# Sixteen experts on one core: fixed program order for experts 0 to 14, overflow branch in front of the first

## The chip, the core and the metric

The kernel runs on one core of a Trainium2 chip. The metric is device time in us for one launch, both layers. An engine is named as the profile names it: PE is TensorE (PEld its weight loads), ACT ScalarE, DVE VectorE, POOL GpSimd, SP SyncE, which here only issues transfers; a q behind a name is that engine's sequencer.

## What is computed

The reference is a trunk of two layers over 512 positions of width 1024, in float32. Each layer has a mixer (projections, attention to 256 memory tokens, an output projection, a norm) and then a mixture of 16 experts, of which each position uses two, and a second norm:

```
for i in range(DEPTH):
    ...
    x = layer_norm(ALPHA * x + o, ln1_g[i], ln1_b[i])
    f = grouped_moe(x, router_w, router_b, w_gate[i], w_up[i], w_down[i])
    x = layer_norm(ALPHA * x + f, ln2_g[i], ln2_b[i])

def grouped_moe(...):
    ...                       # top-2 of 16 experts per position, weights in combine
    for e in range(N_EXPERTS):
        h = jax.nn.silu(xt @ w_gate[e]) * (xt @ w_up[e])      # 1024 -> 512
        out = out + combine[:, e:e + 1] * (h @ w_down[e])     # 512 -> 1024
```

## The kernel before

**Mixer and routing.** Each layer first does its mixer and the routing. Routing leaves on chip, per expert, the rows that it takes (`idxs`, L633), their weights (`gates`, L634), and a count of experts with more than 128 rows (`overflow`, L598: `cnt` on TensorE, then four small operations on VectorE up to `nover`, L609).

**One expert** (`experts`, from L649). GpSimd gathers up to 128 rows of x from HBM (L667, two buffers `xg`). TensorE transposes them (`xtrans`, eight blocks, L676), ScalarE and VectorE split the result into a high and a low part (`split_to`, L207 and L208: `xgt`). `gate_up` makes ga and ua: 48 matmuls in the order ga, ua, ga, ua, twelve each. A product of float32 is three matmuls (`mm3`, L202 to L204): high by high, low weights by high x, high weights by low x. Then silu on ScalarE (L692) and the product with ua on VectorE (L693) give h. `htrans` transposes h (`htr`, L699), splits it (`ht`), and `down` makes 24 matmuls into ya in two halves; each half is scaled by the gate on ScalarE (`evict`, L714) into y, which GpSimd adds to the result in HBM (L663).

In the loop over e, expert e's gate and up stand first, then the transposes of e+1, then the down of e-1, then htr of e. Expert 0 has no down behind its gate and up.

**Weights** (`Stream`). Six loads of 1 MB per expert (gate, up, gate, up and two of down) come through SyncE (L147) into a ring of raw pages, at most four in flight. ScalarE copies a raw page to `high` (L168) and VectorE subtracts (`low`, L169), into a ring of eight split pages, ten from expert 5 on, when the raw pages fall from 11 to 9 in layer 0 and from 13 to 11 in layer 1. A load into a raw page is issued once VectorE's `low` has read what was in it; a split is made once TensorE has used up the pages it goes into.

**What sets the order.** A scheduler puts the instructions of each engine into a sequence, by its own model of their times. An engine works its sequence off in order, so an instruction that waits holds up all that stand behind it on that engine.

**The branch** (`more`, L886 on). An expert with more than 128 rows gets the rest of them in a loop under `tc.If(n > 0)`; n is `nover`. All five engines load the number (L889) and compare it (L890); those that skip the body catch up on its semaphores. In the executions shown here the body was not run. Before, the call stands in the loop behind gate and up of expert 0, the transposes of expert 1 and the gather of expert 3; it has a page `rest` of its own.

The functions that the diff touches:

## Time and profile before

| what | value |
|---|---|
| median of 3 runs | 1063.36 us (1061.95 to 1065.77) |
| the profiled execution | 1063.26 us, span 1061.6 us |
| mean granted TensorE clock | 0.970 |
| first ga of the experts in layer 0, in layer 1 | 219.41 us, 733.36 us |

The span runs from the first to the last instruction on the chip; the execution's own time is 1.7 us longer. All times of the rows below are counted from the span's start. Matmuls are pipelined: how far apart two of them start says what one costs, and a matmul's own duration is longer.

### The profile page before, as it was taken

What the parts mean: (1) busy time and instruction counts of PE and PEld (TensorE: products, weight loads), DVE (VectorE), ACT (ScalarE), POOL (GpSimd) and SP (SyncE); (2) the same over time, 40 slices, a digit from 0 to 9 for tenths busy, and PEclk for the clock granted to TensorE, in tenths of its full rate; (3) what the DMA queues carried; (4) which work ended last, traced back from release to release, by engine and by line L of the source; (5) the groups of instructions that cost most, each with busy time, mean ns of one, the idle gap of its engine ahead of it and who ended that gap; (6) DMA issues with size and microseconds to landing.
All of it is one profiled execution on the core that took longest, in us unless ns stands there. A gap on an engine that the chain in (4) does not pass through costs nothing. (4 is left out here: it accounts for less than half of the span.)

```text
span 1061.6 us, 12769 instructions
## 1 busy us (share of the span) xinstructions
PE 991.3 (93%) x4815; PEld 812.6 (77%) x4816; DVE 780.7 (74%) x880; ACT 628.6 (59%) x682; POOL 170.8 (16%) x115
## 2 busy tenths in 40 slices
PE   8999999769999999899899999986699999998995
PEld 6788889658888887678679887875588888886873
DVE  4638667866889976788794656475789999777885
ACT  4526533446788865767653514232688888767762
POOL 0000004311222212101101000212022222221123
PEclk9999999979999999999999999986899999999998
DMA  9713358568999999999690414492499999999934
GB/s 323 274 41 119 120 198 296 181 224 287 361 371 307 396 350 330 319 319 338 175 390 26 159 51 159 148 390 74 172 362 349 371 341 376 354 356 335 333 67 157
DMA packets 102220, 273.31 MB, mean 257 GB/s; under 512 B 10442, under 2 KB 10966, under 8 KB 102152
## 3 DMA queue, kind: packets, MB, share of 16 engines
q1 hardware_dynamic: 89480, 242.84, 62.8%
q0 software_dynamic: 11808, 26.97, 9.1%
q10 hardware_dynamic: 864, 2.62, 0.7%
q8 instruction: 39, 0.64, 0.2%
q14 instruction: 29, 0.24, 0.1%
HBM read 262.22 MB, written 26.21 MB: 272 GB/s over the span
## 5 line engine op out<-in xcount | busy, mean ns | idle before, releaser
L169 DVE TENSOR_TENSOR low<-raw,high 128x2048 fp32r<-128x2048 f32 x189 | 429.8, 2290 | 90.6 <-ACT high L168 87.2
L168 ACT ACTIVATE high<-raw 128x2048 fp32r<-128x2048 f32 x189 | 358.2, 1913 | 44.8 <-PE ga L204 33.4
L168 ACT ACTIVATE split<-raw 128x1024 fp32r<-128x1024 f32 x66 | 68.5, 1058 | 76.5 <-PE za L204 26.0
L203 PE MATMUL ua<-low,xgt 128*128 128x512 f32 x248 | 97.8, 394 | 9.0 <-DVE low L169 9.0
L202 PE MATMUL ya<-high,ht 128*128 128x512 f32 x256 | 103.5, 406 | 1.3 <-ACT high L168 1.3
L203 PE MATMUL ya<-low,ht 128*128 128x512 f32 x256 | 102.3, 400 | 2.1 <-DVE low L169 2.1
L204 PE MATMUL ya<-high,ht 128*128 128x512 f32 x256 | 101.8, 398 | 0.8 <-DVE ht L208 0.7
L203 PE MATMUL ga<-low,xgt 128*128 128x512 f32 x248 | 99.9, 403 | 2.1 <-DVE low L169 1.9
L202 PE MATMUL ga<-high,xgt 128*128 128x512 f32 x248 | 100.4, 405 | 0.0
L204 PE MATMUL ga<-high,xgt 128*128 128x512 f32 x248 | 98.1, 396 | 0.0
L169 DVE TENSOR_TENSOR split<-raw,split 128x1024 fp32r<-128x1024 f32 x57 | 68.7, 1221 | 39.7 <-ACT split L168 38.9
L202 PE MATMUL ua<-high,xgt 128*128 128x512 f32 x248 | 97.4, 393 | 0.1
L204 PE MATMUL ua<-high,xgt 128*128 128x512 f32 x248 | 96.9, 391 | 0.0
L667 POOL DMA_INDIRECT xg<-x1d,idxs x32 | 49.8, 1556 | 267.6 <-PE xt L676 238.3
L169 POOL TENSOR_TENSOR split<-raw,split 128x1024 fp32r<-128x1024 f32 x9 | 21.7, 2406 | 284.8 <-DVE sto L474 148.9
L207 ACT ACTIVATE xgt<-xt 128x512 fp32r<-128x512 f32 x64 | 36.4, 592 | 50.3 <-PE ua L203 26.0
L202 PE MATMUL za<-xh,split 128*128 128x512 f32 x160 | 61.9, 393 | 2.0 <-ACT xh L207 2.0
L203 PEld LDWEIGHTS ua<-low,xgt 128*128 128x128 f32 x248 | 46.6, 188 | 21.0 <-DVE low L169 11.7
L203 PE MATMUL za<-xl,split 128*128 128x512 f32 x160 | 62.5, 391 | 0.0
L204 PE MATMUL za<-xh,split 128*128 128x512 f32 x160 | 61.5, 390 | 0.0
L203 PEld LDWEIGHTS ya<-low,ht 128*128 128x128 f32 x256 | 48.6, 190 | 13.7 <-DVE low L169 3.1
L202 PEld LDWEIGHTS ya<-high,ht 128*128 128x128 f32 x256 | 48.6, 190 | 12.9 <-ACT high L168 1.8
(250 smaller groups left out, 1899.1 us busy)
## 6 DMA issues: line engine op xcount, KB each, us to landing
raw<-in_w_gate_dram SPq DMA_DIRECT2D x64, 1024.0 KB, 8.8
raw<-in_w_up_dram SPq DMA_DIRECT2D x64, 1024.0 KB, 8.3
raw<-in_w_down_dram SPq DMA_DIRECT2D x64, 1024.0 KB, 9.5
raw<-in_w_kv_dram SPq DMA_DIRECT2D x8, 1024.0 KB, 7.0
raw<-in_w_out_dram SPq DMA_DIRECT2D x8, 1024.0 KB, 6.1
raw<-in_w_in_b_dram SPq DMA_DIRECT2D x8, 1024.0 KB, 10.2
raw<-in_w_in_a_dram SPq DMA_DIRECT2D x6, 1024.0 KB, 5.5
x1d<-x POOLq DMA_DIRECT2D x8, 512.0 KB, 5.8
```

What stands on the lines that cost most here:

```text
L168: act.activation(high, src, AF.Copy)
L169: (pool_e if self.on_pool(self.count) else vec).tensor_tensor(low, src, high, op=OP.subtract)
L202: pe.matmul(o, a[0], b[0], start=start, stop=False)
L203: pe.matmul(o, a[0], b[1], start=False, stop=False)
L204: return pe.matmul(o, a[1], b[0], start=False, stop=stop)
L207: r = act.activation(hi, src, AF.Copy)
L667: pool_e.indirect_dma_start(out=xg[:, e % 2], out_offset=None, in_=x1d[i], in_offset=bass.IndirectOffsetOnAxis(ap=tabs[e][0], axis=0), bou ...
```

## The change

The call of `more` moves to a place ahead of the rings, the first transposes and the loop; instead of the page `rest` it uses the page `hy`, which the experts write later. In the loop, TensorE, ScalarE and VectorE work experts 0 to 14 in the order in which the program is written (`tc.manual_schedule`); before the last expert's gate and up the scheduler takes over again. So that the written order is usable, three pieces change place in the program: silu stands behind the last release of ga's pages, the product ahead of the last release of ua's (a release is what emits the next split), and the eviction of a half of down ahead of the release of its last page.

```diff
--- before.py
+++ after.py
@@ -688,9 +688,11 @@
                             k = 4 * half + 2 * j + kk
                             m = mm3(a[u], (xt[:, 0, k, :], xt[:, 1, k, :]), (g[:, 0, kk, :], g[:, 1, kk, :]),
                                     k == 0, k == KB - 1)
+                        if half and u and j:
+                            vec.tensor_tensor(hp[:, 1, :], hp[:, 0, :], a[1], op=OP.mult)
                         W.done(g)
-            act.activation(hp[:, 0, :], a[0], AF.Silu)
-            vec.tensor_tensor(hp[:, 1, :], hp[:, 0, :], a[1], op=OP.mult)
+                    if half and not u:
+                        act.activation(hp[:, 0, :], a[0], AF.Silu)
             return m
 
         def htrans(e):
@@ -707,8 +709,9 @@
                     for kk in range(2):
                         k = 2 * j + kk
                         mm3(o, (ht[:, 0, k, :], ht[:, 1, k, :]), (g[:, 0, kk, :], g[:, 1, kk, :]), k == 0, k == 3)
+                    if j:
+                        evict(n, o)
                     W.done(g)
-                evict(n, o)
 
         def scaled(e):
             return lambda n, o: act.activation(ys[e % 2][:, n * 512:(n + 1) * 512], o, AF.Copy, scale=tabs[e][1])
@@ -719,23 +722,23 @@
             with tc.issue_after(last_entry[-1]):
                 keep_warm(8)
         fill()
-        rest = page("more", [P, 4, FE])
+        more(i, hy)
         W.keep, W.flight = 0, 4
         W.ahead, W.whole, W.on_pool = 6, True, lambda n: False
         W.rings(8)
         W.pump()
         xtrans(0)
         gather(2)
+        order = ExitStack()
+        order.enter_context(tc.manual_schedule(engines={ET.PE, ET.Activation, ET.DVE}))
         for e in range(E):
+            if e == last:
+                order.close()
             up = gate_up(e, (lambda: (down(last - 1, scaled(last - 1)), scatter(last - 1))) if e == last else None)
             if e + 1 < E:
                 xtrans(e + 1)
             if e + 3 < E:
                 gather(e + 3)
-            if e == 0:
-                more(i, rest)
-                drop(rest)
-                W.pump()
             if e == 5:
                 W.parts += 2
             if 0 < e < last:
```

**VectorE in layer 0, ahead of the first expert** (`split` is a half page of the mixer's last weights, `low` the low part of an expert's weights, `vt` a part of attention's values). Before:

```order
L169 TENSOR_TENSOR split_1868<-raw_1225,split_1868 128x1024
L208 TENSOR_TENSOR vt_1701<-va,vt_1701 128x512
L633 TENSOR_SCALAR idxs<-tab 128x16
L634 TENSOR_REDUCE gates<-tab 128x16
L604 TENSOR_TENSOR ovf<-cnt,thr 1x48
L607 TENSOR_REDUCE ovn<-ovf 1x1
L608 CAST flags<-ovf 1x48
L609 CAST nover<-ovn 1x1
L169 TENSOR_TENSOR low_1931<-raw_1310,high_1930 128x2048
L208 TENSOR_TENSOR vt_1701<-va,vt_1701 128x512
L169 TENSOR_TENSOR low_1894<-raw_1254,high_1893 128x2048
L208 TENSOR_TENSOR xgt_1693<-xt,xgt_1693 128x512 x2
```

and now:

```order
L169 TENSOR_TENSOR split_1868<-raw_1225,split_1868 128x1024
L169 TENSOR_TENSOR low_2040<-raw_1254,high_2039 128x2048
L633 TENSOR_SCALAR idxs<-tab 128x16
L634 TENSOR_REDUCE gates<-tab 128x16
L208 TENSOR_TENSOR vt_1701<-va,vt_1701 128x512 x2
L169 TENSOR_TENSOR low_2081<-raw_1310,high_2080 128x2048
L604 TENSOR_TENSOR ovf<-cnt,thr 1x48
L607 TENSOR_REDUCE ovn<-ovf 1x1
L608 CAST flags<-ovf 1x48
L609 CAST nover<-ovn 1x1
L892 TENSOR_LOAD nover
```

The two splits of expert weights stood behind `nover`; one of them now stands ahead of `idxs`, the other ahead of the count.

**TensorE in layer 0 where the branch was, behind expert 0's gate and up.** Before, the first and the last rows of the branch:

```order
L204 MATMUL ua<-high_1930,xgt_1693 128x512
L676 MATMUL xt<-ident,xg_1690 128x128 x4
L889 TENSOR_LOAD nover
L890 COMPARE_AND_BRANCH
...
L890 UNCONDITIONAL_BRANCH
L699 MATMUL htr<-ident,h_1692 128x128 x4
L202 MATMUL ga<-high_1948,xgt_1693 128x512
```

and now:

```order
L204 MATMUL ua<-high_2080,xgt_1693 128x512
L676 MATMUL xt<-ident,xg_1690 128x128 x8
L701 MATMUL htr<-ident,h_1692 128x128 x4
L202 MATMUL ga<-high_2098,xgt_1693 128x512
L203 MATMUL ga<-low_2099,xgt_1693 128x512
```

The load of `nover` and the branch left this place (they stand ahead of expert 0's eight transposes now), and all eight transposes of expert 1 stand here, where four of them stood earlier.

**ScalarE in layer 0 at experts 10 and 11** (the rows of before are those at 441 to 462 us). Before:

```order
L714 ACTIVATE h_1692<-ya,gates 128x512
L168 ACTIVATE high_3659<-raw_3466 128x2048
L207 ACTIVATE ht<-htr 128x512
L714 ACTIVATE h_1692<-ya,gates 128x512
L168 ACTIVATE high_3697<-raw_3484 128x2048
L168 ACTIVATE high_3717<-raw_3502 128x2048
L168 ACTIVATE high_3748<-raw_3520 128x2048
L207 ACTIVATE xgt_1693<-xt 128x512
L168 ACTIVATE high_3766<-raw_3558 128x2048
L692 ACTIVATE h_1692<-ga 128x512
L207 ACTIVATE xgt_1693<-xt 128x512
L168 ACTIVATE high_3784<-raw_3578 128x2048
```

and now, for one expert:

```order
L717 ACTIVATE h_1692<-ya,gates 128x512
L168 ACTIVATE high_3699<-raw_3485 128x2048
L717 ACTIVATE h_1692<-ya,gates 128x512
L168 ACTIVATE high_3719<-raw_3503 128x2048
L207 ACTIVATE ht<-htr 128x512
L168 ACTIVATE high_3749<-raw_3523 128x2048
L168 ACTIVATE high_3767<-raw_3560 128x2048
L168 ACTIVATE high_3785<-raw_3580 128x2048
L695 ACTIVATE h_1692<-ga 128x512
L168 ACTIVATE high_3805<-raw_3610 128x2048
L207 ACTIVATE xgt_1693<-xt 128x512 x2
```

Between two evictions stands one split, and `ht` comes behind both; the order is the same for each expert. VectorE's order follows it: six splits, the product and `ht` between one expert's `xgt` and the next's.

## Rows read from the trace of the kernel before

**Rows 1.** The page's table of engines: busy us, share of the span, instructions.

```profile
PE 991.3 (93%) x4815; PEld 812.6 (77%) x4816; DVE 780.7 (74%) x880; ACT 628.6 (59%) x682; POOL 170.8 (16%) x115
```

**Rows 2.** Busy time by stage in layer 0's expert loop (from:to in us, length; then busy us and instructions of TensorE, its weight loads, VectorE, ScalarE and GpSimd, the granted clock, the DMA engines' busy share, GB/s).

```profile
340.00:400.00 60.00, 60.00 (x284) 49.70 (x283) 50.73 (x34) 45.47 (x40) 13.93 (x7) 1.00 1.01 369
420.00:480.00 60.00, 53.97 (x244) 42.46 (x244) 44.80 (x27) 43.00 (x36) 6.82 (x5) 1.00 0.95 320
```

**Rows 3.** TensorE in layer 0 around its first expert, in order of time (start, duration, both us; in brackets the idle time before it and what ended it; a matmul's duration reaches into the next one's).

```profile
214.19 1.95 PE L676 MATMUL xt<-ident,xg 128*128 128x128 f32 x8 [3.87 <-DMA xg<-x1d,idxs]
...
219.41 0.77 PE L202 MATMUL ga<-split,xgt 128*128 128x512 f32 x1
...
231.74 0.63 PE L676 MATMUL xt<-ident,xg 128*128 128x128 f32 x4
237.97 1.09 PE L699 MATMUL htr<-ident,h 128*128 128x128 f32 x4 [5.59 <-DVEq L890]
238.71 0.78 PE L202 MATMUL ga<-high,xgt 128*128 128x512 f32 x1
```

**Rows 4.** The same in layer 1.

```profile
730.90 2.81 PE L676 MATMUL xt<-ident,xg 128*128 128x128 f32 x12 [1.96 <-DMA xg<-x1d,idxs]
733.36 0.78 PE L202 MATMUL ga<-split,xgt 128*128 128x512 f32 x1
...
754.41 1.09 PE L699 MATMUL htr<-ident,h 128*128 128x128 f32 x4 [7.14 <-DVEq L890]
```

**Rows 5.** The chain that ended last, behind the branch of layer 1 (start, us, what; here a matmul's time is the distance to the next).

```profile
755.50 0.43 PE ga L202
...
758.84 0.23 PE ga L202
```

**Rows 6.** What TensorE waited for in 240 to 512 (the first two rows) and in 755 to 1010 (the last two): us in total, times, longest.

```profile
PE ua L203 <- DVE low L169: 5.1, 3, 1.8
...
PE ya L202 <- ACT high L168: 1.3, 1, 1.3
...
PE ua L203 <- DVE low L169: 2.7, 2, 1.7
PE ga L203 <- DVE low L169: 1.0, 2, 0.5
```

**Rows 7.** VectorE and GpSimd ahead of layer 0's first expert: the table of rows, the count of overflows, the first gather.

```profile
209.75 0.16 DVE L633 TENSOR_SCALAR idxs<-tab 128x16 int32<-128x16 f32 x1
...
210.81 0.14 DVE L609 CAST nover<-ovn 1x1 int32<-1x1 f32 x1
...
210.20 1.09 POOL L667 DMA_INDIRECT xg<-x1d,idxs  x1 [1.15 <-DVE gates L634]
```

**Rows 8.** The branch's own instructions in both layers, on TensorE and SyncE (durations in ns: least, median, most; start of the first and of the last), and SyncE's next weight load behind it in layer 0.

```profile
L889 PEldq TENSOR_LOAD <-nover x2: 315/403/491, 228.6 to 744.5; - x2
...
L889 SPq TENSOR_LOAD <-nover x2: 283/372/462, 237.6 to 729.7; - x2
...
L890 PEldq COMPARE_BRANCH  x2: 318/336/353, 229.2 to 745.0; - x2
...
243.18 0.38 SPq L147 DMA_DIRECT2D raw<-in_w_up_dram  x1
```

**Rows 9.** ScalarE in layer 1 during the first expert: the second split, and the table load ahead of silu.

```profile
740.19 1.92 ACT L168 ACTIVATE high<-raw 128x2048 fp32r<-128x2048 f32 x1 [0.33 <-DVE low L169]
...
744.74 1.28 ACT L692 ACT_TABLE_LOAD   x1
```

**Rows 10.** Groups of ScalarE and VectorE in 240 to 510 (count; busy us, mean ns; idle time before them and what ended it).

```profile
L168 ACT ACTIVATE high<-raw 128x2048 fp32r<-128x2048 f32 x84 | 159.0, 1913 | 18.2 <-PE ga L204 13.3 <-PE ua L204 4.9
...
L714 ACT ACTIVATE h<-ya,gates 128x512 f32<-128x512 f32 x14 | 9.6, 689 | 7.6 <-PE ya L204 7.6
...
L169 DVE TENSOR_TENSOR low<-raw,high 128x2048 fp32r<-128x2048 f32 x83 | 188.6, 2290 | 40.6 <-ACT high L168 39.0 <-DMA raw<-in_w_gate_dram 0.8 <-DMA raw<-in_w_down_dram 0.5
L208 DVE TENSOR_TENSOR xgt<-xt,xgt 128x512 fp32r<-128x512 f32 x28 | 18.6, 684 | 0.7 <-ACT xgt L207 0.7
```

**Rows 11.** Transfers: in 340 to 400 the queue of the weight loads (packets, MB, share of 16 engines) and one kind of load (count, KB each, median us to landing), in 430 to 480 another kind, in 850 to 950 all packets and the queue of the weight loads.

```profile
q1 hardware_dynamic: 6702, 19.93, 87.9%
...
raw<-in_w_up_dram SPq DMA_DIRECT2D x6, 1024.0 KB, 11.5
...
raw<-in_w_down_dram SPq DMA_DIRECT2D x6, 1024.0 KB, 7.1
...
DMA packets 12601, 35.79 MB, mean 358 GB/s; under 512 B 1318, under 2 KB 1318, under 8 KB 12595
...
q1 hardware_dynamic: 10867, 32.04, 86.1%
```

**Rows 12.** ScalarE in layer 0 around 446, in order of time.

```profile
445.62 0.60 ACT L207 ACTIVATE ht<-htr 128x512 fp32r<-128x512 f32 x1 [1.90 <-PE ya L203]
...
446.69 5.51 ACT L168 ACTIVATE high<-raw 128x2048 fp32r<-128x2048 f32 x3
```

**Rows 13.** TensorE's htr of three experts of layer 0, six experts apart.

```profile
276.08 0.60 PE L699 MATMUL htr<-ident,h 128*128 128x128 f32 x4
...
383.82 0.60 PE L699 MATMUL htr<-ident,h 128*128 128x128 f32 x4
...
501.56 0.60 PE L699 MATMUL htr<-ident,h 128*128 128x128 f32 x4
```

## The prediction

> **What bounds the kernel now.** I read the views from coarse to fine. The engine table [rows 1] says that TensorE is busy 93% of the span, so a change can only win where TensorE stands idle or runs at its lower clock; VectorE at 74% is next. The table by stage [rows 2] shows where that is inside the expert loops: TensorE is busy for all of 340–400 and for 53.97 of 60 in 420–480, at the same work a little later. The TensorE timelines [rows 3, 4] give the two big holes a name: htr of expert 0 stands 5.59 us (layer 0) and 7.14 us (layer 1) behind VectorE's sequencer at L890, the overflow branch. The chain behind the second hole [rows 5] shows what follows it: matmuls 0.43 apart, then 0.23 apart, so TensorE came out of the hole at 1.2 GHz. The table of waits [rows 6] names the small holes: in 240–512 and again in 755–1010 it stood behind weight splits (`low` on VectorE, `high` on ScalarE), up to 1.8 us at a time. So TensorE's own work is the bound, with holes in it, and the change bears on both kinds.
>
> **The branch.** Before, every engine leaves expert 0's work, loads the count, compares, meets the others and only then goes on. Removing it behind expert 0 frees htr. What it cost in layer 0: the hole of 5.59, and after it ten matmuls at 0.43 instead of 0.23, 2.0 us. The next expert's first ga began at 238.71 and was, at full clock, worth 240.7. In layer 1 htr began at 754.41 and ga 0.74 later, as in layer 0, with seven slow matmuls, 1.4 us: worth 756.6 [rows 4, 5].
>
> What the branch costs in its new place, layer 0: it needs `nover`, made at 210.81 now [rows 7]. In the new order VectorE has a `low` (2.29, [rows 10]) ahead of idxs and another ahead of ovf, with two vt (0.68) between. Before, one vt stood ahead of idxs and the two lows behind nover. I add: the first low can begin about 209 when its high is done, idxs ends near 211.5 instead of 209.9; vt twice to 212.7; the second low to 215; four small operations, 0.14 to 0.2 each, to about 215.9. The gather starts behind gates, 1.6 later, but lands before that: it took from 210.20 until the transposes began at 214.19, so now until 215.6. After nover, TensorE pays load and compare, 0.32 to 0.49 and 0.34 [rows 8], so xt begins at about 217 instead of 214.19. Before, ga still had to wait for the second gather, since four transposes of expert 1 stood ahead of it, and began at 219.41 [rows 3]. In layer 1 ga began 2.46 after the first xt (730.90 to 733.36); 217 + 2.5 gives ga at 219.5. Nothing is lost at the front. Layer 1: the small operations are done ahead of the first xt, which waited 1.96 for its gather [rows 4]; load and compare (0.83 at most) fit in there, and ga stays at 733.4, give or take 1. A table load of ScalarE behind the branch (1.28, [rows 9]) lies beside xt.
>
> Behind expert 0 no down stands between its gate/up and expert 1's. TensorE ends ua at 231.8, transposes eight blocks (twice the 0.63 for four, [rows 3]) to 233.0 and does htr after the product (0.68). Then ga of expert 1 needs `xgt`, and on VectorE a low (2.29) stands ahead of the two xgt parts (0.68 each): ga ends twelve matmuls ahead of ua, at 229.0, silu at 229.6, the next high at 231.6; product to 232.5, low to 234.8, xgt to 235.5 and 236. The first two matmuls of ga need only the high part, so its start is worth 235.3. **Gain in layer 0: 240.7 − 235.3 = 5.4.**
>
> Layer 1 has five lows in this place, and some highs that wait for the low before them, as now at 740.19 [rows 9]. Ga's first page comes free near 735.5: low to 737.8, high to 739.7, low to 742, high to 743.9, low to 746.2, low to 748.5, product to 749.2; silu and a table load (1.28) stand ahead of the last high, so the last low ends near 751.6 and xgt at 752.3 and 753. TensorE, done with 48 matmuls and xt at about 746, has two holes of 2.5 to 3.5. A hole of 3.87 behind little work left the first xt at the lower clock (1.95 for eight against 0.63 for four, [rows 3]), so I charge 1.3 for slow matmuls: worth 753.6. **Gain in layer 1: 756.6 − 753.6 = 3.0**, between 0 (another low late) and 4.3 (no slow clock). If this cover is gone, ga(1) is what is late, not htr.
>
> Layer 1's weight loads now start when VectorE frees the first page behind the branch, near 748; before, SyncE stood at the branch until VectorE was through, which let htr go at 754.4.
>
> **The splits.** The holes of [rows 6] are no late loads: high's idle time ends by ga and ua of TensorE, and low's 40.6 us by high, only 1.3 of it by DMA [rows 10]. A load issued into the page that a split has just freed is split eight splits later, 8 × 17.96/6 = 23.9 us, and landed in 7 us in 430–480 [rows 11]: it lay there some 17 us. What is wrong is ScalarE's order: by 445.62 it has idled 1.90 for an ht that TensorE let go only behind a piece of ya; then it evicts, and only at 446.69 does it begin three highs in a row [rows 12], and the low that TensorE needs comes up to 1.8 late [rows 6]. The new order sets one high between two evictions. The price is read from htr, which comes once per expert [rows 13]: 276.08 to 383.82 holds six periods in 107.74, 17.96 each, and 383.82 to 501.56 six in 117.74: **10.0 us, plus the 1.3 that a ya waited for a high after that [rows 6], 11.3 in layer 0**; in layer 1 I take the idle sum, 2.7 + 1.0 = 3.7 [rows 6].
>
> Does the new order keep the clean period? VectorE per expert: 6 × 2.29 + 0.68 + 3 × 0.685 = 16.5; ScalarE: 6 × 1.91 + 4 × 0.60 + 2 × 0.69 = 15.2. The tightest way begins at an expert's first ga: 15.0 us to the end of its first ya (60 matmuls at 0.23, [rows 5], and the transposes), then on VectorE's order eviction 0.69, high 1.91, six lows 13.7, ht, product and two xgt 2.7, and 0.4 of waiting for the second high: 34.4, and the ga two experts later starts after 35.9. So 1.5 to spare, and no wait by this sum.
>
> Loads: with TensorE never idle six must land in 17.96, one per 2.99. When DMA was full, the loads' queue moved 32.04 MB in 100 us (850–950) and 19.93 MB in 60 (340–400) [rows 11]; at 1.049 MB a load that is one per 3.27 and per 3.16. In layer 0 a load then landed in about 12, so lay 12 ahead, and a split is itself ready some 4 us before its use. Seven more experts lose 42 × 0.17 = 7 us of that stock, or 42 × 0.28 = 12 at the slower rate: I charge 1.0, bounds 0 and 3. Layer 1's loads start some 6 us earlier than now; it pays nothing.
>
> **Sum.** Layer 0: 5.4 + 11.3 − 1.0 = 15.7. Layer 1: 3.0 + 3.7 = 6.7. Together 22.4 off the profiled execution's 1063.26, which stands 0.1 under the median of the runs: **1041**. Own range 1034 to 1047: the front ±2, layer 1's seam +1.3/−3, loads +1/−2.
>
> **Rivals.**
> 1. *The loads become the bound.* For it: a load per 3.27, 19.6 per expert, and a DMA share of 1.01 in 340–400 [rows 2, 11]. Against: the splits waited for TensorE, not for DMA [rows 10]. It decides if the stock of 12 us is used up by expert 8; then seven experts lose 7 × 1.64 = 11.5 in layer 0, what the splits cost there now, and only the branch and layer 1 gain: 1063.3 − 5.4 − 6.7 + 0.2 = **1051**. The Trainium skill (DMA: Bandwidth & Descriptors, "Where 436 GB/s comes from") gives about 358 GB/s as HBM's limit for one core; the trace agrees within 3%: 358 in 850–950 and 369 in 340–400 [rows 2, 11]. By that rule, with all traffic counted (35.79 MB for 30.6 loads), an expert would take an estimated 19.6 us as soon as the stock is gone.
> 2. *The fixed order puts a wait on VectorE* (slower). Place: each `low` waits in program order for its high, with nothing to be done meanwhile. Price: now 40.6 us over 83 lows, 0.49 each [rows 10]; if six per expert keep it, VectorE needs 16.5 + 2.9 = 19.4 per expert, 1.4 over the period, 28 times: 1041 + 39 = **1080**. It begins to cost at 0.24 per low (16.5 + 6 × 0.24 = 17.96) and turns the sign where the waits pass 0.37 per low (16.5 + 6 × 0.37 = 18.7). Against: most of the present waits are on highs that stand in ScalarE behind its own waits.
> 3. *The branch's hole only moves to the front.* For it: SyncE took from 237.6 (its load of nover) to 243.18 (its next weight load) [rows 8]. If TensorE has to wait for as much in layer 0, xt begins at 215.9 + 5.6 = 221.5 and ga at 224, 4.5 late: **1046**. Against: htr began at 237.97 [rows 3], 5 us before SyncE was through.
>
> **Chances.** The forecast 0.70, rival 3 0.08, rival 1 0.12, rival 2 0.10. 0.3%, or 3.2 us, is about what a measurement of this kernel can tell from no change. Of rival 2 some 0.01 falls inside that (small waits), and of the others 0.04, where several bounds meet: faster 0.86, within 0.05, slower 0.09. The range 1034 to 1056 reaches over rivals 3 and 1, with the 5 us that several bounds together may add to them, and leaves out most of rival 2.
>
> **What would show it.** Right: htr of expert 0 without L893 behind it, near 233 and 749; the first ga of layer 0 near 219.5; htr every 18.0 us from expert 2 to 14 in both layers; TensorE busy for all of 420–480; no split among TensorE's waits over 1 us in total per layer. Wrong: a period over 18.3; `low` waits with ga or ua behind them, or a `raw` that ends high's idle time (rival 1); a hole ahead of the first xt longer than 6 us; layer 1's ga(1) after 755.

## The result, and the profile after it

The changed kernel takes **1034.03 us** (median of 4 runs, 1032.77 to 1034.84); beside it the kernel before took 1064.57. The ratio is 0.9707, with a 95% interval from 0.9668 to 0.9745. Forecast were 1041 and a range from 1034 to 1056: the direction was right, the gain forecast was too small by about 8 us, and the time stands at the very edge of the range. The profiled execution took 1033.29 us, its span is 1031.5.

The engine table of the page, beside [rows 1]: TensorE works 95% of a span that is 30 us shorter.

```profile
PE 982.3 (95%) x4815; PEld 810.1 (79%) x4816; DVE 776.2 (75%) x880; ACT 627.5 (61%) x684; POOL 214.0 (21%) x115
```

The table by stage, with the columns of [rows 2]; the second window is 20 us longer than there, the third is in layer 1.

```profile
340.00:400.00 60.00, 60.00 (x283) 49.75 (x282) 51.51 (x33) 49.07 (x42) 19.59 (x7) 1.00 1.03 374
400.00:480.00 80.00, 80.00 (x378) 66.52 (x377) 71.52 (x46) 64.77 (x55) 19.57 (x7) 1.00 1.01 357
850.00:950.00 100.00, 100.00 (x472) 82.96 (x472) 87.27 (x57) 79.41 (x68) 34.12 (x12) 1.00 1.01 368
```

TensorE stands still nowhere in these windows, where before it lost 6 of 60 us in 420 to 480. Of all that [rows 6] list, one wait is left in layer 0 between 225 and 512, and it belongs to the seam between experts 0 and 1 (waits of TensorE: us, times, longest):

```profile
PE ga L204 <- DVE xgt L208: 1.7, 1, 1.7
```

TensorE at that seam, beside [rows 3], with the columns of that group:

```profile
217.36 1.95 PE L676 MATMUL xt<-ident,xg 128*128 128x128 f32 x8 [5.42 <-DMA xg<-x1d,idxs]
219.14 0.79 PE L202 MATMUL ga<-split,xgt 128*128 128x512 f32 x1
...
231.14 1.11 PE L676 MATMUL xt<-ident,xg 128*128 128x128 f32 x8
232.15 0.66 PE L701 MATMUL htr<-ident,h 128*128 128x128 f32 x4
232.87 0.50 PE L202 MATMUL ga<-high,xgt 128*128 128x512 f32 x1
...
235.31 0.50 PE L204 MATMUL ga<-high,xgt 128*128 128x512 f32 x1 [1.71 <-DVE xgt L208]
```

The hole of 5.59 is gone. The transposes, htr and two matmuls of ga follow one another, and the third waits for xgt behind a low, as forecast (233, and 235.3 to 235.5). The same in layer 1, beside [rows 4]:

```profile
708.90 1.70 PE L676 MATMUL xt<-ident,xg 128*128 128x128 f32 x8 [2.45 <-DMA xg<-x1d,idxs]
710.43 0.79 PE L202 MATMUL ga<-split,xgt 128*128 128x512 f32 x1
...
727.24 1.11 PE L701 MATMUL htr<-ident,h 128*128 128x128 f32 x4 [3.52 <-DVE h L692]
728.01 0.78 PE L202 MATMUL ga<-high,xgt 128*128 128x512 f32 x1
...
730.37 0.80 PE L204 MATMUL ga<-high,xgt 128*128 128x512 f32 x1 [1.16 <-DVE xgt L208]
```

htr waits 3.52 for the product, which stands behind VectorE's splits, and what follows runs at the lower clock (transposes in 1.11 instead of 0.66). Seen from the layer's first ga it comes 16.8 after it (15.6 forecast), and the third matmul of ga(1) 19.9 after it (18.9 to 19.6 forecast).

**Where the 30 us came from.** I laid marks of equal work side by side: points behind which both kernels have the same matmuls to do. htr of one expert is such a mark only where the same ya stand ahead of it. All gains in us:

| stretch | before | after | gain | forecast |
|---|---|---|---|---|
| layer 0: start to first ga | 219.41 | 219.14 | 0.3 | 0 |
| first ga to htr of expert 2 | 56.67 | 51.19 | 5.5 | 5.4 |
| htr of 2 to htr of 8 | 107.74 | 107.46 | 0.3 | 0 |
| htr of 8 to the last ya | 151.01 | 134.06 | **17.0** | **10.3** |
| layer 1: first ga to htr of 2 | 58.77 | 56.27 | 2.5 | 3.0 |
| htr of 2 to the last ya | 246.57 | 241.99 | 4.6 | 3.7 |

All other stretches hold 0.1. One row is off by much: experts 9 to 15 of layer 0. Here are its marks before, the ga that begin experts 9 and 15, and the matmuls ahead of them (TensorE in order of time; the htr between is the last of [rows 13]):

```profile
383.59 0.40 PE L204 MATMUL ya<-high,ht 128*128 128x512 f32 x1
...
384.18 0.48 PE L202 MATMUL ga<-high,xgt 128*128 128x512 f32 x1
...
416.45 0.55 PE L203 MATMUL ya<-low,ht 128*128 128x512 f32 x1 [1.83 <-DVE low L169]
416.79 0.63 PE L204 MATMUL ya<-high,ht 128*128 128x512 f32 x1
417.22 0.63 PE L202 MATMUL ya<-high,ht 128*128 128x512 f32 x1
...
501.91 0.48 PE L203 MATMUL ya<-low,ht 128*128 128x512 f32 x1
...
504.33 0.39 PE L204 MATMUL ya<-high,ht 128*128 128x512 f32 x1
504.56 0.39 PE L202 MATMUL ga<-high,xgt 128*128 128x512 f32 x1
...
509.35 0.49 PE L202 MATMUL ya<-high,ht 128*128 128x512 f32 x1 [1.30 <-ACT high L168]
...
526.62 0.66 PE L699 MATMUL htr<-ident,h 128*128 128x128 f32 x4 [0.96 <-DVE h L693]
529.43 0.50 PE L204 MATMUL ya<-high,ht 128*128 128x512 f32 x1 [0.73 <-DVE ht L208]
```

and after:

```profile
378.14 0.48 PE L202 MATMUL ga<-high,xgt 128*128 128x512 f32 x1
...
485.02 0.39 PE L204 MATMUL ya<-high,ht 128*128 128x512 f32 x1
485.25 0.60 PE L701 MATMUL htr<-ident,h 128*128 128x128 f32 x4
485.61 0.48 PE L202 MATMUL ga<-high,xgt 128*128 128x512 f32 x1
```

At 383.82 all of a down stood ahead of htr, at 501.56 eleven of its 24 ya (501.91 to 504.33) still came behind it. The scheduler had moved htr forward, and so the distance between the two htr, 117.74, left out 2.6 us of work that its six experts still owed. From ga to ga it is 120.38 before and 107.47 after: **12.9** saved, not 10.0. Expert 15, from its ga to the last ya, took 30.27 before and 26.24 after: **4.0** saved, through all three waits in the rows above. The stretches between these marks as windows of each kernel show that the waits are not the whole (columns of [rows 2]), before:

```profile
384.18:504.56 120.38, 112.05 (x508) 89.87 (x506) 92.89 (x59) 83.03 (x71) 17.27 (x10) 0.99 0.95 329
504.56:534.83 30.27, 27.13 (x118) 19.80 (x117) 23.09 (x18) 20.71 (x17) 4.84 (x4) 1.00 0.67 205
```

and after:

```profile
378.14:485.61 107.47, 107.47 (x508) 89.19 (x506) 94.74 (x61) 86.21 (x73) 27.78 (x10) 1.00 1.01 360
485.61:511.85 26.24, 26.19 (x120) 19.99 (x118) 22.96 (x18) 17.86 (x15) 6.20 (x4) 1.00 0.84 275
```

With the same 508 records TensorE was busy 112.05 before and 107.47 after. The idle time is 120.38 − 112.05 = 8.3 of the 12.9; the other 4.6 are counted as busy. They lie in what a hole does to the matmuls around it: the modelled end of the last one (0.39) reaches 0.16 past its pace of 0.23, the first one behind takes 0.34, and behind the hole at 416.45 eight followed 0.43 apart, the pace of 1.2 GHz (the granted clock is 0.50 in 416.76 to 420). For the ten holes that the trace shows between these two ga that makes 10 × 0.27 + 8 × 0.20 = 4.3.

### The profile page after: what moved, and what is told of

Same layout as the page of the kernel before. It is cut to its first block, busy times and chain, and to the rows that moved or that the text cites. A ratio compares the mean times of both kernels' runs of the same rounds, so it can differ in the third digit from the quotient of the medians.

```text
span 1031.5 us, 12728 instructions
## 1 busy us (share of the span) xinstructions
PE 982.3 (95%) x4815; PEld 810.1 (79%) x4816; DVE 776.2 (75%) x880; ACT 627.5 (61%) x684; POOL 214.0 (21%) x115
## 5 line engine op out<-in xcount | busy, mean ns | idle before, releaser
L667 POOL DMA_INDIRECT xg<-x1d,idxs x32 | 87.1, 2722 | 272.1 <-PE xt L676 262.0
L203 PE MATMUL ga<-low,xgt 128*128 128x512 f32 x248 | 97.7, 394 | 0.0
L663 POOL DMA_INDIRECT rd<-h,idxs x16 | 40.4, 2528 | 89.1 <-ACT h L717 89.1
L204 PEld LDWEIGHTS ya<-high,ht 128*128 128x128 f32 x256 | 48.1, 188 | 12.8 <-DVE ht L208 1.3
L204 PEld LDWEIGHTS ga<-high,xgt 128*128 128x128 f32 x248 | 46.9, 189 | 13.9 <-DVE xgt L208 4.0
L202 PEld LDWEIGHTS ya<-high,ht 128*128 128x128 f32 x256 | 48.4, 189 | 10.6 <-ACT ht L207 0.6
## 6 DMA issues: line engine op xcount, KB each, us to landing
raw<-in_w_down_dram SPq DMA_DIRECT2D x64, 1024.0 KB, 10.4
```

The costliest lines, as they stand in the source:

```text
L202: pe.matmul(o, a[0], b[0], start=start, stop=False)
L203: pe.matmul(o, a[0], b[1], start=False, stop=False)
L204: return pe.matmul(o, a[1], b[0], start=False, stop=stop)
L663: added[e] = pool_e.indirect_dma_start(out=rd[i], out_offset=bass.IndirectOffsetOnAxis(ap=tabs[e][0], axis=0), in_=ys[e % 2], in_offset=No ...
L667: pool_e.indirect_dma_start(out=xg[:, e % 2], out_offset=None, in_=x1d[i], in_offset=bass.IndirectOffsetOnAxis(ap=tabs[e][0], axis=0), bou ...
```

## The experiments

My theory after the result: the two edits gain separately, the branch at the seams and the fixed order everywhere else; the forecast failed in the price of layer 0's splits. Against it stood that one edit brings the other's gain (expert 15 freed by the branch's move), that the three moved pieces and not the fixed order take the waits away, and that TensorE is now held by something else, VectorE or the loads. I name runs by their labels. Every ratio is to the kernel before, run beside them.

**The two edits apart.** The branch alone is the kernel before with these edits:

```diff
-        rest = page("more", [P, 4, FE])
+        more(i, hy)
...
-                more(i, rest)
-                drop(rest)
```

> The kernel before with only the branch moved to the front (with the page hy); the scheduler orders the experts, silu, product and eviction stand where they stood. Theory: the two parts of the change add up, and the branch is worth its two seams alone, 5.8 us in layer 0 and 2.5 in layer 1: 1064.6 - 8.3 = 1056; layer 0's experts 9 to 15 keep their waits for splits, some 16 us over the fixed order. Rival: the branch, by holding up SyncE and the loads, also made the later waits; then most of the 30 us come with it alone, 1040 or less.

Measured 1057.08, ratio 0.9944 (0.9924 to 0.9964). First ga to htr of 2 takes 50.22 in layer 0 and 55.59 in layer 1, even less than after, though the first ga comes later behind the routing (table below); htr of 8 to the last ya takes 149.5 in layer 0, nearly as before, and in layer 1 143.6, which is 5 more than before and gives the seam's gain there back. TensorE's waits in layer 0 between 240 and 528 are those of [rows 6] and of the htr and ya above:

```profile
PE ua L203 <- DVE low L169: 5.4, 4, 1.8
PE ga L203 <- DVE low L169: 1.4, 3, 0.5
PE ya L202 <- ACT high L168: 1.3, 1, 1.3
PE htr L699 <- DVE h L693: 1.0, 1, 1.0
PE ya L204 <- DVE ht L208: 0.7, 1, 0.7
```

So moving the branch takes away none of the split waits, nor expert 15's.

The order alone is the changed kernel with the branch back in the loop behind expert 0, and with its own page:

```diff
-        more(i, hy)
+        rest = page("more", [P, 4, FE])
...
+            if e == 0:
+                more(i, rest)
+                drop(rest)
+                W.pump()
```

> The changed kernel with the branch put back behind expert 0's gate and up, with its own page. Theory: 1034.0 + 8.3 = 1042; htr of expert 0 waits 5 to 8 us for the branch in each layer, and every later expert takes 17.9. Rival (the later waits came from the branch): 1050 or more, with waits for splits at TensorE behind expert 8 in layer 0.

Measured 1038.96, ratio 0.978 (0.9758 to 0.9802). Periods are 17.91, htr of 8 to the last ya 134.05: all of the 17 us belong to the order. htr(0) waits for the branch again, in layer 1 for

```profile
  DVEq L897: 9.9, 1
```

(us, times), and first ga to htr of 2 takes 63.74 there instead of 56.27. In layer 0 the first ga comes at 213.88, 5.3 ahead of after, with the gather issued at 208.28 instead of 211.78. The two ratios add up to 2.8% of gain, both edits together gave 2.9%.

By place they do not add up. The stretch from the last matmul of the routing's table (`tab`, L626) to htr of 2 takes in the front and the seam (us; with the branch alone, five or six ga of expert 3, 1.1 to 1.4 us of work, already lie ahead of that htr):

| layer | before | branch alone | order alone | both |
|---|---|---|---|---|
| 0 | 67.1 | 63.7 | 60.8 | 61.6 |
| 1 | 67.1 | 63.9 | 71.2 | 63.9 |

In layer 0 the order alone reaches htr of 2 as early as both edits do, although its htr(0) still waits 3.45 for the branch: its first ga stands behind eight transposes instead of twelve and comes 6.8 behind the table instead of 10.4. In layer 1 the order alone loses 4.1, and the branch's move gives 7.3 on top of it. So the seam's gain is the branch's in layer 1 only; in layer 0 the two edits overlap.

**Which part of the order.** Silu, product and eviction put back into their old places:

```diff
-                        if half and u and j:
-                            vec.tensor_tensor(hp[:, 1, :], hp[:, 0, :], a[1], op=OP.mult)
                         W.done(g)
-                    if half and not u:
-                        act.activation(hp[:, 0, :], a[0], AF.Silu)
+            act.activation(hp[:, 0, :], a[0], AF.Silu)
+            vec.tensor_tensor(hp[:, 1, :], hp[:, 0, :], a[1], op=OP.mult)
...
-                    if j:
-                        evict(n, o)
                     W.done(g)
+                evict(n, o)
```

> The changed kernel with silu, product and eviction written where they stood before (behind all of gate and up, behind the last release of down), the order still fixed. Theory: what counts is that no split stands behind a wait for TensorE that comes late; with splits ahead of evictions the chain has the same slack of about 1.5 us, so 1034 with at most 3 more. Rival: a split has to stand between the two evictions; without the three moves the waits come back, 0.5 us or more per expert, 1048 or more.

Measured 1033.43, ratio 0.9719 (0.9699 to 0.9739), which the changed kernel's interval covers: the three moves are worth nothing by themselves. Then the fixed order entered only at expert 9:

```diff
-        order.enter_context(tc.manual_schedule(engines={ET.PE, ET.Activation, ET.DVE}))
         for e in range(E):
+            if e == 9:
+                order.enter_context(tc.manual_schedule(engines={ET.PE, ET.Activation, ET.DVE}))
```

> The changed kernel with the fixed order for experts 9 to 14 only; experts 0 to 8 are left to the scheduler. Theory: the scheduler's order of experts 2 to 8 cost 0.05 us per expert and no more, so 1034 to 1036. Rival: the late experts run without waits because the early ones left them a better stock of splits and loads; then some of the 13 us of experts 9 to 14 come back, 1040 or more.

Measured 1034.26, ratio 0.9724 (0.9704 to 0.9745), the same again. The scheduler's order costs nothing in experts 0 to 8 that these runs can tell (some 3 us); what is won lies behind them. That bears out where the prediction looked (around 446) and leaves its price to be explained. That it is ScalarE's order, as the prediction says, is argued and not shown: the edit fixes three engines at once, and from expert 10 on the scheduler had also put htr into the middle of the down ahead of it.

**How much room VectorE has** (rival 2). One instruction of 0.69 us more per expert on VectorE (the edit reaches expert 15 too), then four (`range(4)`):

```diff
         split_to(ht)
+            for _ in range(1):
+                vec.tensor_tensor(ht[:, 1], t, ht[:, 0], op=OP.subtract)
```

> The changed kernel with the second half of ht's split done twice on VectorE for experts 0 to 14 (0.60 to 0.68 us more per expert, same result). Theory: the fixed order has about 1.5 us to spare in two experts on VectorE's way, 0.75 per expert, so this still hides: 1034, at most 3 more. Rival: VectorE's order is already the bound, each extra 0.65 shows 28 times: 1052.

> The same with four extra times (2.4 to 2.7 us more per expert). Theory: of two experts' 4.8 to 5.4 us some 1.5 to 2.2 hide, so each expert takes 1.3 to 2.0 longer, 1070 to 1088, with TensorE waiting for xgt or a low once per expert. Rival: VectorE has more room than the sum says (it idles 1.4 us and more per expert that could be filled): under 1050.

One: measured 1044.38, ratio 0.9793 (0.9765 to 0.9821), not the 1034 expected. Yet the periods of experts 2 to 14 stay at 17.91 and 17.93. The loss lies at the ends, most of it behind htr of 14: from there to the last ya it takes 31.56 instead of 26.60 in layer 0 and 31.70 instead of 27.07 in layer 1. Four: 1111.07, ratio 1.0425 (1.0391 to 1.046), above what I expected, with a period of 19.95 and TensorE behind splits in nearly every expert (layer 0, 245 to 500):

```profile
PE ua L203 <- DVE low L169: 21.0, 12, 1.8
```

Four add 2.76 per expert and the period grows by 2.04, so VectorE's room is 0.7 us per expert: 1.4 per two, the 1.5 that the prediction worked out. What room there is lies in VectorE's waits for a high: 14.3 us in the six experts from htr of 2 to htr of 8 in layer 0 of the changed kernel, 8.8 with one instruction more, 8.3 with four. The rest of the second run's loss lies again behind htr of 14: 39.33 in layer 0 and 36.08 in layer 1.

**Where expert 15 pays.** Either the scheduler, which takes over at expert 15, orders it badly, or VectorE comes there with a backlog. First the fixed order through to the end (its close stands behind the loop now), with one more instruction each:

```diff
-            if e == last:
-                order.close()
...
+        order.close()
```

> The run with ht's low part made twice (1044 us), now with the fixed order through expert 15 as well. In that run experts 2 to 14 took 17.91 as ever and expert 15 took 4 us longer in each layer. Theory: the 10 us came from the scheduler's other plan for expert 15 and the seams, not from VectorE's load; with expert 15 in program order some 8 of them go: 1034 to 1037. Rival: VectorE ends the loop with a backlog that expert 15 pays: 1042 to 1045 again.

Measured 1043.71, ratio 0.9787 (0.9749 to 0.9825), no better. From htr of 14 to the last ya it takes 33.93 and 31.58, now with TensorE's selt (the matrix that picks expert 15's rows for the final sum) waiting for VectorE (layer 0):

```profile
PE selt L758 <- DVE selt L755: 4.8, 1, 4.8
```

In program order VectorE makes selt only behind the lows of expert 15. So this order is a bad one for expert 15, and the run does not tell a backlog from an order; the same order without the extra instruction was not run.

Then the extra instruction in experts 0 to 8 alone (`if 0 <= e < 9`), and in 9 to 14 alone:

> The changed kernel with ht's low part made twice in experts 0 to 8 only. Theory (backlog): VectorE has caught up by expert 14, expert 15 takes what it takes in the changed kernel, 1034 to 1036. Rival (the scheduler plans expert 15 otherwise whenever the loop differs): 4 us more in each layer, 1041 to 1045.

> The same in experts 9 to 14 only. Theory (backlog): VectorE comes to expert 15 as late as in the run with the extra work in all experts, so 4 us more in each layer: 1041 to 1044. Rival: six experts' extra work is too little to show, 1034 to 1036.

0 to 8: 1038.8, ratio 0.975 (0.9705 to 0.9796), the end at 26.60 and 27.07 as without it. 9 to 14: 1041.5, ratio 0.9788 (0.9747 to 0.9829), the end at 30.83 and 29.37, in layer 0 with the wait

```profile
PE ya L203 <- DVE low L169: 2.1, 1, 2.1
```

The intervals of the two overlap; the places of the loss do not. The times alone would fit a backlog, but the traces do not show one. VectorE's low at htr of 14 and ScalarE's highs after it, in layer 0, in the changed kernel (its htr of 14 stands at 485.25):

```profile
485.18 2.29 DVE L169 TENSOR_TENSOR low<-raw,high 128x2048 fp32r<-128x2048 f32 x1 [1.62 <-ACT high L168]
488.32 3.72 ACT L168 ACTIVATE high<-raw 128x2048 fp32r<-128x2048 f32 x2
```

and with 9 to 14 (htr of 14 at 485.19):

```profile
485.12 2.29 DVE L169 TENSOR_TENSOR low<-raw,high 128x2048 fp32r<-128x2048 f32 x1 [0.89 <-ACT high L168]
488.26 7.51 ACT L168 ACTIVATE high<-raw 128x2048 fp32r<-128x2048 f32 x4
```

VectorE begins that low at the same place in both, 0.07 ahead of htr, and had been idle before it: it brings no lag to expert 15. What differs is the scheduler's sequence there. ScalarE makes four highs in a row ahead of the next eviction instead of two, and TensorE has 3 of the down's ya ahead of its next ga instead of 13. The run with one instruction in every expert has the same 3 and 4; the run with 0 to 8 has 13 and 2, as in the changed kernel. In layer 1 the runs part in the same way. So what the traces show is the rival of these two expectations, that the scheduler plans expert 15 otherwise, in the two runs that lose time there; why it does is open. Whether the waits 0.96 and 0.73 of VectorE in expert 15 before come from the sequence too is not shown.

The run with 0 to 8 loses its 5 us at layer 0's front (first ga at 220.84, with the routing's table 1.7 later) and between htr of 0 and of 1 (21.88 instead of 20.27, in layer 1 22.93 instead of 21.54). The extra instruction need not be the cause: e7_keep3 below, which has none, takes 21.87 and 22.90 there. What parts these executions is TensorE's clock (last section).

**Are the loads the bound?** (rival 1) Three raw pages kept empty:

```diff
-        W.keep, W.flight = 0, 4
+        W.keep, W.flight = 3, 4
```

> The changed kernel with three raw pages fewer in the expert loop (8 to 6 in layer 0, 10 to 8 in layer 1 behind expert 5). In the changed kernel the last loads of layer 0's loop lie 4 to 7 us ready before their split, in layer 1 9 us. Theory: that stock is what three pages, 9 us, take away, so layer 0 loses 1 to 5 us behind expert 9 and layer 1 at most 1: 1035 to 1040, with splits waiting for DMA. Rival A: loads are not near the bound, 1034. Rival B: loads are the bound from there on, 9 us or more per layer, 1052.

Measured 1035.71, ratio 0.9733 (0.9698 to 0.9768). But the edit took no page away. Counted from a load's issue to the end of its low, the run holds 10.95 raw pages on average in 240 to 330 and 8.95 in 345 to 400, the changed kernel 10.92 and 8.91, with the same 11 and 9 at most: pages are handed out in turn, and the edit only moves a load's place in the program. So this run tests nothing, and what is known of the loads comes from the changed kernel itself. TensorE is busy for all of the three windows of the table above, and in layer 0 behind 437 a load has lain landed for 2.4 to 6.8 us before its split (2.7 to 6.2 in this run): the loads are not the bound. They come near it, as what their issues on SyncE wait for tells. 400 to 480, before:

```profile
SPq L147 <- DVE low L169: 70.6, 23, 6.1
```

and after:

```profile
SPq L147 <- DMA raw<-in_w_up_dram: 25.4, 9, 4.5
...
SPq L147 <- DVE low L169: 1.9, 4, 1.0
```

Before, a load waited for its page; now four are in flight and it waits for one to land (for gate and down 22.7 and 19.2 more), so pages no longer set the stock there. DMA runs at a share of 1.01, and the stock, the time that a load lies landed, shrinks (19.6 us at 277, 12.7 at 349, 2.4 at 474, at the same place in an expert each time), but the loop ends before it is gone. The Trainium skill (DMA: Bandwidth & Descriptors, "Where 436 GB/s comes from") puts HBM's limit for one core at about 358 GB/s. Here 60 us at 374 and 100 us at 368 were moved, so by measurement it is not a wall at that figure. Nor does a share above 1.00 say that little more is to be had: in 670 to 696, with writes among the loads, the changed kernel moved 404 GB/s at a share of 1.03.

**Does the branch cost anything in front?** (rival 3) The changed kernel without `more(i, hy)`; it leaves out the rows of an expert beyond 128:

> The changed kernel without the branch at all: the handling of experts with over 128 rows is left out (none of the inputs needs it). It measures what the branch still costs in front. Theory: in layer 0 the first ga comes at 213.9, as it did with the fixed order and the branch behind expert 0, instead of 219.1; in layer 1 only a table load and two hand-overs go, 0 to 1.5: 1034.0 - 5.2 - 0.8 = 1028. Rival: the gathers set the start of the first transposes in front, so that the branch costs nothing there: 1032 to 1034.

Measured 1034.63, ratio 0.9703 (0.9662 to 0.9745), where I expected 1028: the branch in front costs nothing that these runs can tell. The gather is issued at 212.03 without it, no earlier, and the first transposes wait for it as long (us, times):

```profile
  DMA xg<-x1d,idxs: 5.6, 1
```

So the prediction's 217 and 219.5 came true by another cause. It had `nover` and the branch as the last thing before the transposes, with the gather landed at 215.6. In fact `nover` was there at 215.36, and the gather, issued at 211.78, landed at 217.22.

**Could the seam give more?** In layer 1 htr(0) waits 3.52 for the product, which stands behind splits. Four tries. First ten split pages from the start of layer 1:

```diff
-        W.ahead, W.whole, W.on_pool = 6, True, lambda n: False
-        W.rings(8)
+        W.ahead, W.whole, W.on_pool = 8 if i else 6, True, lambda n: False
+        W.rings(10 if i else 8)
...
-            if e == 5:
+            if e == 5 and not i:
```

> The changed kernel with ten split pages from the start in layer 1 (instead of eight, ten from expert 5) and eight halves split ahead. Theory: in layer 1 TensorE's waits behind expert 0 (3.5 for the product, 1.2 for xgt, slow matmuls after it) come from highs that wait for a low to free a page; with two more pages the product comes about 3 us earlier: 1030 to 1031. Rival: the number of lows ahead of the product is what counts, and there is one more now: 1034 to 1036.

Measured 1043.82, ratio 0.9794 (0.9765 to 0.9822), a miss of 14: htr(0) of layer 1 waits (us, times)

```profile
  DVE h L692: 9.7, 1
```

With more pages one more low stands ahead of the product, and in a fixed order VectorE does it first. Second, the fixed order entered ahead of the branch:

> The changed kernel with the fixed order entered ahead of the branch, so that layer 0's first two splits of expert weights stand behind the count and the branch on VectorE and ScalarE instead of ahead of idxs and of the count. Theory: idxs is done 1.6 us earlier, nover 4 us earlier, the first transposes begin when the gather has landed, near 214.5 to 215.5 instead of 217.4, and ga follows: 1031 to 1032. Rival: the splits, now late, hold up xgt or the first gate and up: 1034 or more.

Measured 1036.41, ratio 0.9715 (0.9676 to 0.9754), not 1031. The transposes begin 6.54 behind the routing's table instead of 8.61, but the table itself comes at 210.81, 2.1 later, and first ga to htr of 2 takes 53.19 instead of 51.19. That is the clock again: the hole behind expert 0 is the same 1.71, and the granted clock behind it is 0.50 (236 to 238). So this run does not tell what its edit is worth. Third, the splits of expert 0's last pages held back until the product and xgt are emitted:

```diff
+                        if e == 0 and half and (u == 1 or i):
+                            W.hold = True
...
+            if e == 0:
+                W.hold = False
+                W.pump()
```

> The changed kernel with expert 0's last splits (layer 0: one, layer 1: two) emitted behind its product and the next expert's xgt instead of ahead of them. Theory: TensorE's waits behind expert 0 are for what stands behind those lows in VectorE's order; in layer 1 htr waits about 1 instead of 3.5 and ga 0 to 0.5 instead of 1.2, and the clock stays up, 4 to 5 us; in layer 0 1.7: 1028. Rival: the lows moved back are needed at once by ga and ua of expert 1, so the waits only move: 1033 or more.

Measured **1025.64**, ratio 0.9616 (0.9578 to 0.9654), faster than both kernels. First ga to htr of 2 takes 49.60 in layer 0 and 50.63 in layer 1, 1.6 and 5.6 less than after. VectorE in layer 1 at the seam:

```profile
722.38 0.68 DVE L694 TENSOR_TENSOR h<-h,ua 128x512 f32<-128x512 f32 x1
722.98 1.28 DVE L208 TENSOR_TENSOR xgt<-xt,xgt 128x512 fp32r<-128x512 f32 x2
724.86 4.50 DVE L169 TENSOR_TENSOR low<-raw,high 128x2048 fp32r<-128x2048 f32 x2 [0.60 <-ACT high L168]
```

Product and xgt come together, and the lows behind them. Fourth, the same with the fixed order and the first transposes put ahead of the first expert splits in layer 0 (the rings and the pump behind the gather):

> The run with the product first (1025.6 us), and in layer 0 the fixed order entered ahead of the branch with the first transposes written ahead of the first splits, so that no split of expert weights stands ahead of idxs, the count or xgt, and no weight load is set off by one while the gather runs. Theory (the gather, issued 1.6 us late and slowed from 3.9 to 5.4 us by the loads beside it, holds the first transposes in layer 0): the first transposes begin 4.4 to 5.5 us behind the last routing matmul instead of 8.6, and 2 to 3 us come off: 1023. Rival: the splits, now behind xgt, hold up the second half of gate and up: 1025 or more.

Measured **1023.86**, ratio 0.9627 (0.9584 to 0.967). The transposes begin 6.48 behind the table; but the ratio does not tell it from the third.

## Why the prediction was right or wrong

- **What bounds the kernel**: right. TensorE's own work with holes in it, and the change took nearly all holes out.
- **The branch, layer 0, 5.4**: measured 5.5, and the order of events at the seam as described. That the numbers agree is in part luck: in e7_keep3, with the same written order, the clock fell behind the hole and the stretch took 53.45, a gain of 3.2; and the order alone reaches htr of 2 as early as both edits, so that the 5.5 is not shown to be the branch's. The front lost nothing, as said, but the reason was the gather, not the branch.
- **The branch, layer 1, 3.0**: measured 2.5, with htr's hole 3.52 in place of 2.5 to 3.5, and ga's 1.16.
- **The splits, layer 1, 3.7**: measured 4.6, of which experts 2 to 8 gave 0.2 (0.7 by their htr, but two ga, 0.45 us of work, lay ahead of htr of 8 before).
- **The splits, layer 0, 11.3: here it failed.** The place was right, and so was the fixed order as what takes these waits away; the size was not: 17.0 measured. The step read the price "from htr, which comes once per expert"; but the scheduler had moved the last htr ahead of eleven ya, which hides 2.6, and the clean period was 0.05 shorter than assumed (0.3). The step also priced expert 15 by one wait of 1.3, where the kernel before lost 4.0 there: two waits for VectorE (0.96 and 0.73) lay in the trace and were not counted, and each hole costs more than its idle time. Together 2.9 and 2.7, the second being 4.0 less 1.3.
- **The loads, 1.0**: not due. No wait came of it, although the stock shrank by the 7 to 12 us named (12.7 at 349 to 2.4 at 474, seven experts on). 2.9, 2.7 and 1.0 make up 6.6 of the 6.7 in that row. Had these stood in the sum, it would have been 1034 to 1035.
- **Rival 1** didn't come: TensorE waits for no split, and no load lands late for its split. **Rival 2** didn't come, though its condition did: in layer 0, from htr of 2 to htr of 8, each low still waits 0.40 for its high (14.3 over 36), past the 0.24 from which that rival was to cost and the 0.37 at which it was to turn the sign. VectorE is busy 15.8 per expert there, not the 16.5 of the sum, and its waits give way to work. What the extra instructions bear out is the other sum, 1.5 to spare in two experts (0.7 per expert measured). **Rival 3** didn't come: the branch in front costs nothing.

Open: which engine's order makes the waits of layer 0; why the scheduler plans expert 15 otherwise when expert 14 has one instruction more; why the mixer's end differs by up to 3.8 us between these kernels (the routing's table at 207.0 to 210.8); and whether the fourth try is worth more than the third.

## To carry to other kernels

Take a stage's gain between points of equal work, and check at both ends what stands ahead of the mark: a scheduler may have moved the mark itself. A fixed order is worth what the waits behind the scheduler's order cost, plus what each hole does to the matmuls after it; it has to be written so that a short operation on the path (product, xgt) does not stand behind long ones that nobody waits for yet. When a run loses time where the scheduler takes over, compare its sequences there before calling the loss a backlog. And count in the trace that an edit did what it was meant to do (here: the raw pages held) before reading anything from its time.

## What the runs showed of the hardware

From the first gather's start in layer 0 to the transposes that wait for it 3.99 us passed before [rows 3, 7], and 5.58 after, where loads of 1 MB were issued ahead of it and beside it (SyncE, then GpSimd):

```profile
208.95 0.37 SPq L147 DMA_DIRECT2D raw<-in_w_gate_dram  x1
211.44 0.37 SPq L147 DMA_DIRECT2D raw<-in_w_up_dram  x1
```

```profile
211.78 1.08 POOL L667 DMA_INDIRECT xg<-x1d,idxs  x1 [2.90 <-DVE gates L634]
```

With the order alone, which issued no load between 200 and 211.34, it was 3.81 (208.28 to 212.09); with the fourth try, and one load at 207.35, 5.22. A small transfer that TensorE waits for seems to pay some 1.5 us for a big one beside it. No run moved the loads alone, so this is read from four kernels and not shown.

At the seam of layer 0 a hole in TensorE's work does not have one price. The wait of 1.71 for xgt, behind the same sequence, is there in the changed kernel and in e7_keep3. In the changed kernel the granted clock stayed at 1.00 behind it (237 to 239); in e7_keep3 it fell to the lower level, 1.2 GHz, and first ga to htr of 2 took 53.45 instead of 51.19 (columns of [rows 2]):

```profile
235.00:237.00 2.00, 2.00 (x6) 1.52 (x6) 2.00 (x2) 0.00 (x0) 0.00 (x0) 0.50 0.76 295
```

So a difference of 2 us at this seam between two profiled executions need not be the work of an edit.
